# Gate products ahead of the query units in the NSA stage of a two-layer hybrid attention kernel

## The chip, the cores and the metric

The program runs on one core of one Trainium2 chip. The metric is the device time of one execution in microseconds (us), given as the median of several runs. The core's engines are TensorE (PE, matrix products; its weight loads are shown as PEld), VectorE (DVE), ScalarE (ACT), GpSimd (POOL) and SyncE (SP, which issues most of the loads). Each engine takes its own instructions strictly in order; semaphores between them are the only coupling.

## What is computed

Two decoder layers on a sequence of 512 tokens of width 1024, in float32. The part of a layer that the change touches:

```python
hn = rms_norm(x, norm_g[0])
(nsa_q, k_c, v_c, k_s, v_s, k_w, v_w, nsa_g, sb_q, sb_k, sb_v, merge_g) = split_columns(hn @ w_in)
kc = compress_blocks(k_c, ...); vc = compress_blocks(v_c, ...)      # gelu(flat @ w1) @ w2
y_nsa = nsa_attention(q_rope, q_plain, kc, vc, ks, vs, kw, vw, gates) @ w_nsa_o
y_sb  = stick_breaking_attention(sb_q, sb_k, sb_v) @ w_sb_o
gate  = jax.nn.sigmoid(merge_g)                                      # 2 * 1024 columns
mixed = (gate[..., :1024] * y_nsa + gate[..., 1024:] * y_sb) @ w_out
x = x + rms_norm(mixed, norm_g[1])
# then a feed-forward block: x = x + rms_norm(square(relu(h @ w_ff1)) @ w_ff2)
```

## The kernel before, in words

Activations lie transposed: 128 channels on the partitions, the 512 tokens along the row. Every float32 product is made of three float32r products: both operands are split into a high and a low part, and `three()` adds hi*hi, hi*lo and lo*hi in one PSUM bank. One output unit of 128 columns of `w_in` is therefore 8 input tiles x 3 = 24 matmuls of 128x512 (`product`, lines 479, 481, 483).

Each unit's weights are 512 KB. `Weight` (lines 145 to 170) loads them with SP into one of **two** raw buffers ("wr", line 149), ACT copies out the high part (L157), and the low part is made in one of two ways: POOL subtracts (L162), or, with `sub="dma"`, ACT writes the negative raw value into the low buffer as well (L159) and POOL issues an accumulating DMA of the same weights onto it (L160). High and low parts have four buffers each. A raw buffer is free again when its low part is made.

A layer runs in four stages. In the **NSA stage** PE works off an attention with small, dependent steps (scores L673/L674, transposes L720, values L735/L736), and a `Filler` puts independent matmuls between them: `fill.add` appends generators, `fill.run(n)` issues the next n filler steps, `fill.later(n, f)` calls f after n more steps, `fill.until(c)` issues steps until c holds. One step of a `product` is one matmul; one step of a compression unit (`ck.steps`, `cv.steps`, called C[0..3] and D[0..3] after `some(...)`, four steps each) is two matmuls of 64x256 (L378/L379). PE is scheduled by hand in exactly this order; the other engines' orders are made by a scheduler at build time.

The first scores wait for the keys K1, K2 (`keys`, L531 to L533) and the rotated queries xr (`queries`, then `stack`, L350/L351). The four score groups h = 0..3 come four heads at a time; two PSUM banks "s" hold them, so h = 2 needs the bank of h = 0 back, which DVE's masking step L679 frees. The filler before held, in this order (`ORD` number 2): C[0], query unit q2, C[1], q3, C[2], C[3], stick-breaking unit h0[0], D[0], D[1], h0[1], D[2], D[3], h0[2], the three units of h1, and the gate units of m = 0 and 1 (two each). 41 steps (`F0`) ran before the first scores. After C[3], `ck_done` sets off the chain of the compressed keys: transposes cmp_t (L389), DVE and ACT steps of a gelu (L392 to L400), the product cmp_o (L409).

The **stick-breaking stage** (L840 on) has the gate units m = 2..5 as filler. In the **merge stage** (L942 to L964) the remaining two pairs, m = 6 and 7, are issued at m = 1 (`GA`) and m = 4 (`GB`) as 48 filler steps each, between the units of the output projection. The feed-forward stage follows.

A gate product's result is multiplied by the norm factor on DVE (L642) into a tile "sig" that lives until the merge stage.

Of the kernel before, what the change touches and what calls it, by code (L numbers as in the profile page):

```python
# [25 lines left out]
P = 128  # L26
T = 512
D = 1024
# [21 lines left out]
def layer_kernel(ctx, tc, xT, pos, gvec, tri, consts, smalls, w_in, w1, w_o, w_out, ff1, ff2, out):  # L50
# [9 lines left out]
    BUFS = {"L": 20, "Q": 12, "P": 12, "pt": 4, "t": 4, "f": 4, "sig": 4, "act": 16, "st": 1, "R": 2}  # L60

    def big(tag, name, dt=F32):
        return sp.tile([P, T], dt, tag=tag, bufs=BUFS[tag], name=name)

# [406 lines left out]
    def layer(l, acts, R, heads):  # L471
# [165 lines left out]
        def gate_project(m):  # L637
            s2 = []

            def take(ps):  # L640
                s = big("L" if 2 <= m < 4 else "P" if 4 <= m < PLAN["GE"] else "sig", "sig")
                V.tensor_tensor(s, ps, R, ALU.mult)  # L642
                s2.append(s)
                sigs[m] = s2
# [154 lines left out]
        def some(gen, n=4):  # L799
# [12 lines left out]
        ORD = [  # L812
            [q2, C[0], q3, C[1], h0[0], C[2], C[3], h0[1], D[0], D[1], h0[2], D[2], D[3]],
            [q2, C[0], q3, C[1], C[2], h0[0], C[3], D[0], h0[1], D[1], D[2], h0[2], D[3]],
            [C[0], q2, C[1], q3, C[2], C[3], h0[0], D[0], D[1], h0[1], D[2], D[3], h0[2]],
            [q2, C[0], C[1], q3, C[2], C[3], h0[0], D[0], D[1], h0[1], D[2], D[3], h0[2]],
            [q2, C[0], h0[0], C[1], C[2], h0[1], C[3], D[0], q3, D[1], D[2], h0[2], D[3]],
            [h0[0], C[0], q2, C[1], C[2], h0[1], C[3], D[0], q3, D[1], D[2], h0[2], D[3]],
            [h0[0], C[0], q2, C[1], C[2], q3, C[3], D[0], h0[1], D[1], D[2], h0[2], D[3]],
        ][PLAN["ORD"]]  # L820
        fill.add(*ORD, *h1, *gate_project(0), *gate_project(1))
# [21 lines left out]
        fill.add(*(p for m in range(2, PLAN["GE"]) for p in gate_project(m)))  # L843
# [101 lines left out]
        for m in range(KT):  # L945
# [15 lines left out]
            for j in ((0, 1, 4, 5) if PLAN["GE"] == 4 else (0, 1, PLAN["GA"]) if PLAN["GE"] == 5 else (PLAN["GA"], PLAN["GB"])):  # L961
                if j == m:
                    fill.add(*gate_project(gates.pop(0)))
                    fill.run(48)  # L964
# [152 lines left out]
```

## Time and profile before

| | us |
|---|---|
| median of 3 runs | 1628.49 (1623.24 to 1630.78) |
| profiled execution, own time | 1626.38 |
| its span from first to last instruction | 1624.4 |
| PE busy | 1534.3 (94% of the span) |
| DVE busy | 870.5 (54%) |
| ACT busy | 747.9 (46%) |
| POOL busy | 768.2 (47%) |

The shares are averages over stages with different limits. PE's granted clock is 1.00 of full speed in most of the span and falls to half in a few short stretches. Times inside a stage are given from the span's start; layer 0's NSA stage begins at about 44 us, layer 1's at about 846 us, and the merge stages lie at about 350 to 405 us and 1150 to 1206 us.

### The profile page before, as it was taken

To read this page: it belongs to the slowest core of one execution; us is meant where nothing else is said; L and a number is where in the kernel's file an instruction comes from. 1 tells how busy PE (TensorE), PEld (TensorE's weight loads), DVE (VectorE), ACT (ScalarE), POOL (GpSimd) and SP (SyncE) were. 2 spreads that over 40 slices of the span, in tenths; PEclk is the share of its full clock that TensorE was granted. 3 is DMA by queue.
4 is the path that set the end of the run, shared out by engine and by line. 5 is a ranking of instruction groups with operands and counts; after the bars stand their busy time and mean duration, and the time that the engine had idled before them with its cause. 6 is when DMAs were issued, how large, how long until landed. Compare 5 with 4: busy or idle time off the path is not lost.

```text
span 1624.4 us, 20692 instructions
## 1 busy us (share of the span) xinstructions
PE 1534.3 (94%) x7810; PEld 1291.3 (79%) x7810; DVE 870.5 (54%) x1495; ACT 747.9 (46%) x1379; POOL 768.2 (47%) x527
## 2 busy tenths in 40 slices
PE   8788999999989999999887899999998999999996
PEld 5566778888988888888885777788878988888886
DVE  7877954354582332323799698534536823232245
ACT  6666755443352332324356677646343523232342
POOL 4762345446544444446546534354565344444452
PEclk9899999999999999999998999999999999999999
DMA  5464212224312322324234622122343133232321
GB/s 185 108 144 97 51 52 69 75 91 143 106 64 95 98 97 95 100 93 131 95 93 108 162 54 53 52 78 65 103 145 113 43 93 101 92 103 91 104 91 52
DMA packets 49331, 153.74 MB, mean 95 GB/s; under 512 B 5952, under 2 KB 12496, under 8 KB 49232
## 3 DMA queue, kind: packets, MB, share of 16 engines
q1 hardware_dynamic: 45888, 140.84, 27.2%
q0 software_dynamic: 3200, 11.55, 4.1%
q8 instruction: 61, 1.00, 0.3%
q14 instruction: 38, 0.31, 0.1%
q10 hardware_dynamic: 144, 0.03, 0.0%
HBM read 148.15 MB, written 4.26 MB: 94 GB/s over the span
## 4 chain that ended last, share of the span: by engine, by line
PE 77%; DVE 14%; ACT 3%; DMA 1%; issue 1%; POOL 0%; DVEq 0%; ACTq 0%; POOLq 0%
PE ff L186 12%; PE ff L185 12%; PE ff L187 12%; PE proj L483 5%; PE proj L479 5%; PE proj L481 5%; DVE P L690 2%; PE tail L187 2%; PE tail L186 2%; PE tail L185 2%; PE p_t L720 2%; DVE pn L291 2%; PE y L185 1%; PE y L187 1%; PE y L186 1%; PE head L185 1%
## 5 line engine op out<-in xcount | busy, mean ns | idle before, releaser
L162 POOL TENSOR_TENSOR w_lo<-w_raw,w_hi 128x1024 fp32r<-128x1024 f32 x204 | 496.7, 2435 | 503.2 <-ACT w_hi L157 483.5
L157 ACT ACTIVATE w_hi<-w_raw 128x1024 fp32r<-128x1024 f32 x226 | 239.1, 1059 | 530.0 <-PE ff L186 370.9
L483 PE MATMUL proj<-ah,w_lo 128*128 128x512 f32 x496 | 197.9, 399 | 1.7 <-POOL w_lo L162 1.7
L481 PE MATMUL proj<-al,w_hi 128*128 128x512 f32 x496 | 197.8, 399 | 0.0
L479 PE MATMUL proj<-ah,w_hi 128*128 128x512 f32 x496 | 196.8, 397 | 0.7 <-ACT w_hi L157 0.7
L185 PE MATMUL ff<-ah,w_hi 128*128 128x512 f32 x448 | 174.3, 389 | 0.0
L186 PE MATMUL ff<-al,w_hi 128*128 128x512 f32 x448 | 174.3, 389 | 0.0
L187 PE MATMUL ff<-ah,w_lo 128*128 128x512 f32 x448 | 174.3, 389 | 0.0
L186 PE MATMUL ff<-hl,w_hi 128*128 128x512 f32 x432 | 168.2, 389 | 0.8 <-DVE hl L181 0.8
L185 PE MATMUL ff<-hh,w_hi 128*128 128x512 f32 x432 | 168.1, 389 | 0.0
L187 PE MATMUL ff<-hh,w_lo 128*128 128x512 f32 x432 | 168.1, 389 | 0.0
L181 DVE TENSOR_TENSOR hl<-relu,hh 128x512 fp32r<-128x512 f32 x64 | 106.6, 1671 | 84.3 <-ACT hh L180 84.0
L483 PEld LDWEIGHTS proj<-ah,w_lo 128*128 128x128 f32 x496 | 94.1, 190 | 18.5 <-POOL w_lo L162 2.1
L479 PEld LDWEIGHTS proj<-ah,w_hi 128*128 128x128 f32 x496 | 94.0, 190 | 17.3 <-ACT w_hi L157 0.9
L481 PEld LDWEIGHTS proj<-al,w_hi 128*128 128x128 f32 x496 | 94.3, 190 | 16.7
L1012 DVE TENSOR_TENSOR ffa<-ff,ffa 128x512 f32<-128x512 f32 x38 | 26.3, 692 | 150.8 <-PE ff L187 150.8
L185 PEld LDWEIGHTS ff<-ah,w_hi 128*128 128x128 f32 x448 | 84.1, 188 | 17.5
L187 PEld LDWEIGHTS ff<-ah,w_lo 128*128 128x128 f32 x448 | 84.1, 188 | 17.5
L186 PEld LDWEIGHTS ff<-al,w_hi 128*128 128x128 f32 x448 | 84.1, 188 | 17.2
L186 PEld LDWEIGHTS ff<-hl,w_hi 128*128 128x128 f32 x432 | 81.1, 188 | 17.9 <-DVE hl L181 1.2
L185 PEld LDWEIGHTS ff<-hh,w_hi 128*128 128x128 f32 x432 | 81.1, 188 | 16.9
L187 PEld LDWEIGHTS ff<-hh,w_lo 128*128 128x128 f32 x432 | 81.1, 188 | 16.8
(311 smaller groups left out, 3431.1 us busy)
## 6 DMA issues: line engine op xcount, KB each, us to landing
w_raw<-in_ff_dram SPq DMA_DIRECT2D x128, 512.0 KB, 3.5
w_raw<-in_w_in_dram SPq DMA_DIRECT2D x69, 512.0 KB, 3.6
w_lo<-in_w_in_dram POOLq DMA_DIRECT2D x18, 512.0 KB, 7.5
w_raw<-in_w_dram SPq DMA_DIRECT2D x16, 512.0 KB, 3.5
w_raw<-in_w_o_dram SPq DMA_DIRECT2D x16, 512.0 KB, 3.5
w_raw<-in_w_out_dram SPq DMA_DIRECT2D x16, 512.0 KB, 3.5
x<-in_xT_dram SPq DMA_DIRECT2D x8, 256.0 KB, 6.5
w_lo<-in_w_dram POOLq DMA_DIRECT2D x4, 512.0 KB, 6.5
```

Source lines behind the costliest of these rows:

```text
L157: S.activation(h, raw, AF.Copy)
L162: (sub or G).tensor_tensor(l, raw, h.bitcast(F32), ALU.subtract)
L181: V.tensor_tensor(lo, src, hi.bitcast(F32), ALU.subtract)
L185: E.matmul(ps, w.hi(k), ah, start=first, stop=False)
L186: E.matmul(ps, w.hi(k), al, start=False, stop=False)
L187: return E.matmul(ps, w.lo(k), ah, start=False, stop=last)
L291: V.scalar_tensor_tensor(t, mixed[k][:, c], gcol(l, n, k), R[:, c], ALU.mult, ALU.mult)
L479: E.matmul(ps, w.hi(k), ah, start=(k == 0), stop=False)
L481: E.matmul(ps, w.hi(k), al, start=False, stop=False)
L483: E.matmul(ps, w.lo(k), ah, start=False, stop=(k == KT - 1))
L690: V.tensor_scalar(pr[h], pr[h], sm4[:, h:h + 1], None, ALU.mult)
L720: E.transpose(pt[:, P * h:P * h + P], pend[j][0][h][:, P * kt:P * kt + P], ident)
```

## The change

The order list is replaced by one fixed order, in which the first gate pair stands ahead of q2 and q3 in the NSA filler, and three gate pairs (m = 0, 1, 2) are in that stage instead of two. 76 filler steps instead of 41 run before the first scores; the items of query tiles 0, 1, 2 of the second head group get one step more each (`FN10` to `FN12`). The stick-breaking stage's filler has m = 3..6, and the merge stage issues one pair only, m = 7, at m = 1. Tiles "sig" get 6 buffers, and which pool a pair's tiles come from changes.

```diff
--- before.py
+++ after.py
@@ -15,9 +15,9 @@
 PSUM = bass.MemoryType.PSUM
 
 PLAN = {
-    "GE": 6, "GA": 1, "GB": 4,
-    "F0": 41, "F2": 5, "F3": 1, "F1": 7, "AH": 7, "BU": 2, "QD": 77, "FS0": 4, "FS1": 4, "FE": 5, "FN00": 5, "FN01": 3, "FN02": 4,
-    "FN03": 7, "FN10": 5, "FN11": 3, "FN12": 3, "FN13": 7, "FNC0": 1, "FNC1": 7, "CK0": 11, "CK1": 24, "CK2": 13,
+    "GE": 7, "GA": 1, "GB": 4,
+    "F0": 76, "F2": 5, "F3": 1, "F1": 7, "AH": 7, "BU": 2, "QD": 77, "FS0": 4, "FS1": 4, "FE": 5, "FN00": 5, "FN01": 3, "FN02": 4,
+    "FN03": 7, "FN10": 6, "FN11": 4, "FN12": 4, "FN13": 7, "FNC0": 1, "FNC1": 7, "CK0": 11, "CK1": 24, "CK2": 13,
     "CK3": 36, "CV0": 13, "CV1": 28, "SC3": 1, "SC2": 2, "R1": 3, "R2": 4, "CKV": 1, "CKM": 2, "CVM": 1, "ORD": 2, "HS": 6, "H0": 2, "HS2": 7, "FQ": 12,
     "CD": 0, "GT": 24,
 }
@@ -57,7 +57,7 @@
     dp = ctx.enter_context(tc.tile_pool(name="dp", bufs=1, space=bass.MemoryType.DRAM))
     xsave = dp.tile([P, KT, T], F32, name="xsave")
 
-    BUFS = {"L": 20, "Q": 12, "P": 12, "pt": 4, "t": 4, "f": 4, "sig": 4, "act": 16, "st": 1, "R": 2}
+    BUFS = {"L": 20, "Q": 12, "P": 12, "pt": 4, "t": 4, "f": 4, "sig": 6, "act": 16, "st": 1, "R": 2}
 
     def big(tag, name, dt=F32):
         return sp.tile([P, T], dt, tag=tag, bufs=BUFS[tag], name=name)
@@ -638,7 +638,7 @@
             s2 = []
 
             def take(ps):
-                s = big("L" if 2 <= m < 4 else "P" if 4 <= m < PLAN["GE"] else "sig", "sig")
+                s = big("L" if m in (3, 6) else "P" if m in (4, 5) else "sig", "sig")
                 V.tensor_tensor(s, ps, R, ALU.mult)
                 s2.append(s)
                 sigs[m] = s2
@@ -809,16 +809,8 @@
         values()
         q2, q3 = product(5, queries), product(6, last_query)
         C, D = [some(cks) for _ in range(4)], [some(cvs) for _ in range(4)]
-        ORD = [
-            [q2, C[0], q3, C[1], h0[0], C[2], C[3], h0[1], D[0], D[1], h0[2], D[2], D[3]],
-            [q2, C[0], q3, C[1], C[2], h0[0], C[3], D[0], h0[1], D[1], D[2], h0[2], D[3]],
-            [C[0], q2, C[1], q3, C[2], C[3], h0[0], D[0], D[1], h0[1], D[2], D[3], h0[2]],
-            [q2, C[0], C[1], q3, C[2], C[3], h0[0], D[0], D[1], h0[1], D[2], D[3], h0[2]],
-            [q2, C[0], h0[0], C[1], C[2], h0[1], C[3], D[0], q3, D[1], D[2], h0[2], D[3]],
-            [h0[0], C[0], q2, C[1], C[2], h0[1], C[3], D[0], q3, D[1], D[2], h0[2], D[3]],
-            [h0[0], C[0], q2, C[1], C[2], q3, C[3], D[0], h0[1], D[1], D[2], h0[2], D[3]],
-        ][PLAN["ORD"]]
-        fill.add(*ORD, *h1, *gate_project(0), *gate_project(1))
+        g0, g1, g2 = (gate_project(m) for m in range(3))
+        fill.add(g0[0], C[0], g0[1], C[1], q2, C[2], C[3], q3, D[0], D[1], h0[0], D[2], D[3], h0[1], g1[0], h0[2], g1[1], *g2, *h1)
         fill.later(PLAN["GT"], gate_rows)
         fill.run(PLAN["F0"])
         for h in range(4):
@@ -840,7 +832,7 @@
             nsa_values(it)
 
         fill.until(lambda: 0 in sb_in)
-        fill.add(*(p for m in range(2, PLAN["GE"]) for p in gate_project(m)))
+        fill.add(*(p for m in range(3, PLAN["GE"]) for p in gate_project(m)))
         blocks = [(h, kb) for h in range(4) for kb in (3, 2, 1, 0)]
         zs, sps, spt, accs, aps = {}, {}, {}, {}, {}
         loc = {0: (0, 0), 1: (1, 0), 3: (1, 384), 2: (2, 0)}
@@ -958,10 +950,9 @@
             mh, ml = big(tg, f"mh{m}", F32R), big(tg, f"ml{m}", F32R)
             split(mh, ml, sig[0])
             merged.append((mh, ml))
-            for j in ((0, 1, 4, 5) if PLAN["GE"] == 4 else (0, 1, PLAN["GA"]) if PLAN["GE"] == 5 else (PLAN["GA"], PLAN["GB"])):
-                if j == m:
-                    fill.add(*gate_project(gates.pop(0)))
-                    fill.run(48)
+            if m == PLAN["GA"]:
+                fill.add(*gate_project(gates.pop(0)))
+                fill.run(48)
         exp_table()
 
         mixed = [big("L", f"mix{m}") for m in range(KT)]
```

What it moves is seen on three places of two engines, all in layer 0; layer 1 has the same orders but for a few neighbours. Names: w_raw and w_hi are a unit's raw weights and high part, w_lo its low part; xr10, xr11 the rotated queries of the second pair of heads; V20, V21 the values; P_... the probabilities of one score group; cmp_hs the compressed keys' hidden layer.

ACT, from the keys to the values. Before, 615 is the high part of q3's weights and 683 that of C[2]'s; those of q2 and C[1] were made earlier:

```order
L533 ACTIVATE K2s_443<-K2s_443 64x512
L157 ACTIVATE w_hi_615<-w_raw_613 128x1024
L571 ACTIVATE qph_507<-q_493 128x512
L157 ACTIVATE w_hi_683<-w_raw_681 128x1024
L533 ACTIVATE K2w_444<-K2w_444 64x512
L350 ACTIVATE xr10_501<-qr_495 64x512
L350 ACTIVATE xr11_504<-qr_495 64x512
L543 ACTIVATE V20_445<-v_t_511 128x4x64
L543 ACTIVATE V21_446<-v_t_511 128x4x64
```

The same place in the change, where 618 and 619 are C[1]'s weights and 634 is the high part of q2's:

```order
L533 ACTIVATE K2s_443<-K2s_443 64x512
L157 ACTIVATE w_hi_618<-w_raw_616 128x1024
L159 ACTIVATE w_lo_619<-w_raw_616 128x1024
L571 ACTIVATE qph_507<-q_493 128x512
L533 ACTIVATE K2w_444<-K2w_444 64x512
L350 ACTIVATE xr10_501<-qr_495 64x512
L350 ACTIVATE xr11_504<-qr_495 64x512
L543 ACTIVATE V20_445<-v_t_511 128x4x64
L157 ACTIVATE w_hi_634<-w_raw_632 128x1024
L543 ACTIVATE V21_446<-v_t_511 128x4x64
```

C[1]'s low part, which goes by way of a POOL DMA, now starts behind the keys, and q2's weights behind xr10, xr11 and V20.

DVE, from the values to the first masking step L679, before:

```order
L544 TENSOR_TENSOR V21_446<-v_t_511,V21_446 128x4x64
L563 TENSOR_TENSOR q_579<-proj5_535,R0_104 128x512
L555 TENSOR_SCALAR gate_440<-gate_440 128x96
L342 STREAM_SHUFFLE rope_sh_582<-q_579 128x512
L556 RECIPROCAL gate_440<-gate_440 128x96
L344 TENSOR_TENSOR rope_sh_582<-rope_sh_582,sinT_331 128x512
L345 TENSOR_TENSOR qr_581<-qr_581,rope_sh_582 128x512
L679 ISA P_633,mx_628<-s_630,cst_68 128x512
```

and in the change:

```order
L642 TENSOR_TENSOR sig_552<-proj19_520,R0_104 128x512
L544 TENSOR_TENSOR V21_446<-v_t_511,V21_446 128x4x64
L555 TENSOR_SCALAR gate_440<-gate_440 128x96
L556 RECIPROCAL gate_440<-gate_440 128x96
L642 TENSOR_TENSOR sig_614<-proj20_582,R0_104 128x512
L679 ISA P_663,mx_658<-s_660,cst_68 128x512
```

The rotation of q2's queries (L342, L344, L345) has gone behind the first L679; two evacuations of gate products (L642) are in front of it.

ACT, a little later in the change, from q2's neighbours to the compressed keys' hidden layer (before, the weights of three units, C[3], h0[0] and D[0], stood between the values and cmp_hs, and two P_ and the rotated queries of q2):

```order
L157 ACTIVATE w_hi_690<-w_raw_688 128x1024
L157 ACTIVATE w_hi_710<-w_raw_708 128x1024
L157 ACTIVATE w_hi_727<-w_raw_725 128x1024
L157 ACTIVATE w_hi_821<-w_raw_819 128x1024
L681 ACTIVATE P_663,sm4_659<-P_663,mx_658 128x512
L159 ACTIVATE w_lo_822<-w_raw_819 128x1024
L571 ACTIVATE qph_684<-q_670 128x512
L157 ACTIVATE w_hi_842<-w_raw_840 128x1024
L681 ACTIVATE P_703,sm4_659<-P_703,mx_658 128x512
L382 ACTIVATE cmp_hs_722<-cmp_h_567 64x256
```

Weights of five units (C[2], C[3], q3, D[0], D[1]) now stand ahead of cmp_hs, which PE's transposes cmp_t wait for.

## Rows read from the trace of the kernel before

**Rows 1.** The page: busy us, share of the span, instructions of each engine.

```profile
PE 1534.3 (94%) x7810; PEld 1291.3 (79%) x7810; DVE 870.5 (54%) x1495; ACT 747.9 (46%) x1379; POOL 768.2 (47%) x527
```

**Rows 2.** PE timeline, layer 0: start us, us; in brackets idle before, releaser.

```profile
39.74 0.39 PE L479 MATMUL proj<-ah,w_hi 128*128 128x512 f32 x1
...
44.28 0.39 PE L483 MATMUL proj<-ah,w_lo 128*128 128x512 f32 x1
...
46.24 0.33 PE L378 MATMUL cmp_h<-w_hi,bhl 128*64 128x256 f32 x1 [1.13 <-ACT gts L519]
...
55.32 0.50 PE L479 MATMUL proj<-ah,w_hi 128*128 128x512 f32 x1 [0.65 <-ACT w_hi L157]
...
57.77 0.50 PE L483 MATMUL proj<-ah,w_lo 128*128 128x512 f32 x1 [1.71 <-POOL w_lo L162]
...
70.88 0.77 PE L673 MATMUL s<-K1s,xr 128*128 128x512 f32 x1 [7.14 <-ACT xr L350]
```

**Rows 3.** DVE timeline, layer 0.

```profile
63.52 0.42 DVE L544 TENSOR_TENSOR V<-v_t,V 128x256 fp32r<-128x256 f32 x1
...
70.05 0.68 DVE L679 CUSTOM_DVE_ANT_0 P<-s,cst 128x512 f32<-128x512 f32 x1
```

**Rows 4.** PE timeline, layer 1.

```profile
849.39 0.33 PE L378 MATMUL cmp_h<-w_hi,bhl 128*64 128x256 f32 x1 [2.33 <-DVE bhl L369]
...
860.91 0.50 PE L674 MATMUL s<-K2s,xr 128*128 128x512 f32 x1 [0.79 <-ACT K2s L533]
...
871.79 0.77 PE L673 MATMUL s<-K1s,xr 128*128 128x512 f32 x1 [6.73 <-DVE mx L679]
...
889.21 1.29 PE L720 MATMUL p_t<-cst,P 128*128 128x128 f32 x4 [2.26 <-DVE P L690]
...
898.29 0.79 PE L736 MATMUL o_nsa<-ptl,V 128*128 128x512 f32 x1 [3.58 <-DVE ptl L181]
```

**Rows 5.** Stretches: us, busy of PE, PEld, DVE, ACT, POOL, granted clock, DMA share, GB/s.

```profile
70.90:77.00 6.10, 6.10 (x23) 5.30 (x24) 5.96 (x10) 5.60 (x11) 4.08 (x3) 0.50 0.53 171
...
871.80:875.70 3.90, 3.90 (x15) 3.50 (x16) 3.70 (x6) 3.85 (x8) 2.18 (x1) 0.50 0.07 27
```

**Rows 6.** ACT timeline, layer 0.

```profile
54.21 1.06 ACT L157 ACTIVATE w_hi<-w_raw 128x1024 fp32r<-128x1024 f32 x1
...
61.31 0.39 ACT L543 ACTIVATE V<-v_t 128x256 fp32r<-128x256 f32 x1
```

**Rows 7.** POOL timeline, one row of each layer.

```profile
55.34 2.37 POOL L162 TENSOR_TENSOR w_lo<-w_raw,w_hi 128x1024 fp32r<-128x1024 f32 x1 [0.55 <-ACT w_hi L157]
...
854.37 1.28 POOL L343 TENSOR_TENSOR qr<-q,cosT 128x512 f32<-128x512 f32 x1 [2.77 <-DVE q L563]
```

**Rows 8.** Tile w_lo, POOL's DMAs issued in 40:50, then in 830:960.

```profile
DMA to landing us min/median/max: 7.5/7.5/7.5
...
DMA to landing us min/median/max: 5.4/7.2/8.9
```

**Rows 9.** The page's DMA issues: KB of each, median us to landing.

```profile
w_raw<-in_w_in_dram SPq DMA_DIRECT2D x69, 512.0 KB, 3.6
```

**Rows 10.** PE timeline, layer 0, around the compressed keys and values.

```profile
91.53 0.50 PE L736 MATMUL o_nsa<-ptl,V 128*128 128x512 f32 x1 [1.76 <-DVE ptl L181]
...
96.50 0.42 PE L409 MATMUL cmp_o<-cmp_ht,sml 128*64 128x32 f32 x4 [3.10 <-DVE ptl L181]
...
128.16 0.38 PE L415 MATMUL cmp_o<-sml,cmp_ht 128*32 128x64 f32 x4 [1.54 <-DVE cmp_ht L400]
...
130.38 0.49 PE L738 MATMUL o_nsa<-pth,vc 32*128 32x512 f32 x1 [1.84 <-DVE vc L418]
```

**Rows 11.** PE timeline, merge stage of layer 0, behind the second gate pair.

```profile
392.42 0.47 PE L185 MATMUL y<-onh,w_hi 128*128 128x512 f32 x1 [0.99 <-DVE sig L955]
```

**Rows 12.** DVE timeline, the same pair of operations in layers 0 and 1.

```profile
82.05 1.67 DVE L690 TENSOR_SCALAR P<-P,sm 128x512 f32<-128x512 f32 x2
...
881.76 7.79 DVE L690 TENSOR_SCALAR P<-P,sm 128x512 f32<-128x512 f32 x2
```

## The prediction

> **What bounds the kernel now.** The page's busy times come first [rows 1]: PE is busy 94% of the span, the next engine 54%. So the time is PE's work plus the gaps in it, and a change of order can only move gaps. The next view is PE's timeline in the NSA stage, read for the brackets, which name each gap and its releaser. In layer 0 the stage loses 1.13 us before the first compression unit, 0.65 and 1.71 us on q3's weights, and 7.14 us before the third score group [rows 2]; layer 1 loses 2.33, 0.79 and 6.73 us at the like places [rows 4]. The large one is the bank of the first group: it is free only when DVE has run L679, at 70.05 + 0.68 = 70.7 us, right where PE goes on at 70.88 [rows 2, 3]. In layer 0 the row names ACT's xr, which happened to end then; layer 1 names DVE's mx itself [rows 4]. DVE is late because q2's evacuation and rotation stand between the values (63.52) and L679 (70.05) [rows 3]. The view of stretches shows what such a gap costs afterwards: PE runs at half clock for 6.1 us behind it in layer 0 and for 3.9 us in layer 1 [rows 5], so half of that, 3.05 and 1.95 us, is lost on top.
>
> **The change, part by part.** *Steps moved.* From the first row to the last of 21 product matmuls PE takes (44.28 - 39.74) / 20 = 0.227 us each [rows 2]. One gate pair is 48 of them, 10.9 us. The merge stage loses one pair per layer, the NSA stage gains one, and the stick-breaking stage has eight products as before. PE's work is the same; what counts is how much of the 10.9 us falls into gaps that were there, and what gaps are new. 35 of the 48 steps go ahead of the first scores and 12 between later items.
>
> *Gaps that go.* The first gate product stands before C[0], so 24 x 0.227 = 5.4 us of work covers the 1.13 and 2.33 us. q2's rotation goes behind the first L679 on DVE; two evacuations of gate products take its place, and PE comes to the scores later, so the third group should find its bank free. Layer 0: 1.13 + 0.65 + 1.71 + 7.14 = 10.6 us, and 3.05 of half clock. Layer 1: 2.33 + 0.79 + 6.73 = 9.9 us, and 1.95.
>
> *New gap 1, C[1].* Its low part comes by a POOL DMA. Without its gap PE would have been at C[0] at 46.24 - 1.13 = 45.1 us; 48 gate steps, C[0] and the gate rows (some 1.7 us) bring it to C[1] at 57.7. On ACT C[1]'s high part stands where one was made at 54.21 [rows 6]; with that (1.06 us) and the copy of the low one (the same size of tile, so taken the same, overlapping a little) the DMA goes out at about 56.2. The one made nearest to it landed after 7.5 us [rows 8]: 63.7, a wait of 6.0 us. In layer 1 PE is there at 849.39 - 2.33 + 12.6 = 859.7; on POOL the DMA stands behind the rotation that ended at 855.6 [rows 7], and at layer 1's median of 7.2 us [rows 8] it lands at 862.8: 3.1 us. With landings from 5.4 to 8.9 us [rows 8] the bounds are 3.9 to 7.4 and 1.3 to 4.8. I take the middle values, each from its own layer.
>
> *New gap 2, half clock behind it.* The nearest rows are waits of 7.14 and 6.73 us, which cost 3.05 and 1.95 [rows 2, 4, 5]. For 6.0 us I take 2.0 and for 3.1 us 1.0; bounds 0 and 3.05.
>
> *New gap 3, the weights' ring and cmp_t.* Two raw buffers mean that a unit's load waits for the low part of the unit two before: 3.6 + 1.06 + 2.37 = 7.0 us for two units [rows 6, 7, 9]. q2's weights now stand behind the values on ACT: 61.31 + 0.39, then 1.06 and 2.37, so its low part is ready at 65.1. PE, through with C[1] at 64.5, hardly waits for it. C[2]'s low part follows at 68.7, C[3]'s at 72.1 and q3's at 75.7. D[1]'s raw load lands 3.6 later at 79.3, its high part is made by 80.4, and behind that stand one P_ and cmp_hs on ACT, about 1.2 us: PE's cmp_t gets its input at 81.6. PE ends its 76 steps at 65.1 + 20 x 0.227 = 69.6, with half clock 71.6; four score groups (8 matmuls) and 23 steps later, 7.0 us, it stands at cmp_t at 78.6. A wait of 3.0 us, taken for both layers since their queues stand alike; bounds 0 (PE is that much later anyway) and 5.
>
> *cmp_o.* It now stands ahead of the first transposes p_t. DVE has the same list to do before it (masks, two pairs of L690, the gelu). Before, PE lost 1.76 + 3.10 = 4.9 us around it in layer 0 [rows 10] and 2.26 + 3.58 = 5.8 in layer 1 [rows 4]. I take 4.9 for both: 0 and -0.9. It can be worse, which is the slow rival.
>
> *The compressed values.* Counted in filler steps behind the first scores their gelu comes at 128 + 13 - 41 = 100 before and 152 + 13 - 76 = 89 now: 11 steps, 2.5 us, earlier against gaps of 1.54 and 1.84 us [rows 10]. I take 2.5 off in layer 0 and nothing in layer 1, whose gaps there I leave as they are.
>
> *Costed at nothing.* Evacuations of the moved gate products: by the order DVE is through the values (63.52) and the gates some 3 us later and has nothing else to do until the scores; without that cover it is two evacuations, each of the size of L679 (0.68 us) [rows 3]. In the merge stage the pair at m = 4 goes with its 10.9 us. The gap of 0.99 us that followed it [rows 11] is a bank waiting for DVE's L955, and is as likely to stay as to go: 0 to -1 per layer. The weights there come one per unit before and after. The gates' two further buffers and the other pools change no wait that I find. The steps that are added between the later items of head group 1 lie where PE has hardly a gap; they cost their 12 x 0.227 us, which is in the sum already.
>
> **The sum.** Layer 0: -10.6 - 3.05 + 6.0 + 2.0 + 3.0 - 2.5 = -5.2. Layer 1: -9.9 - 1.95 + 3.1 + 1.0 + 3.0 - 0.9 = -5.6. Together -10.8 us. The profiled execution took 1626.38 us, so 1615.6; the median is 2.1 above that execution, which gives **1617.7 us**. By the bounds of gaps 1 and 3 this case reaches from 1610 to 1624. 0.5% of the median, about what a measurement can tell from no change, is 8.1 us: the border is at 1620.4.
>
> **A rule against it.** The pair of L690 took 1.67 us in layer 0 and 7.79 in layer 1 [rows 12], so something beside it can hold it up by 6.1 us. The Trainium skill, SBUF — State Buffer, section "SBUF: two separate sides", says that VectorE and GpSimd share a port pair by an exclusive lock: a GpSimd instruction that holds it blocks a two-port VectorE instruction to its end. The two rows agree with it as far as they go. By the bare rule each L690 that meets a weight split would wait up to that split's 2.37 us, and with all four pairs so held the sum would end at 1617.7 + 4 x 2 x 2.37 = 1636.7; I keep 1617.7, because the ring above gives POOL one split of 2.37 us in 3.5 us and so leaves gaps.
>
> **The rivals.**
> - *All the filler is cover* (0.20). C[1] lands as PE comes, and cmp_t and cmp_o find their inputs. Then both layers win the whole pair: 1626.4 - 2 x 10.9 + 2.1 = 1606.7. For it: the gaps that were there (10.6 + 3.05 us in layer 0) are larger than the pair. Against it: C[1]'s DMA can hardly start before 56 us [rows 6].
> - *One wait for another* (0.19). Landings at 8.9 us in layer 1 and likewise 1.4 us later in layer 0, half clock at 3.05 behind both, no gain at the compressed values and at cmp_o: +1.4 + 1.7 + 1.05 + 2.05 + 2.5 + 0.9 = 9.6 us of the 10.8 gone: 1627.3, no change. For it: each new gap stands where a chain of DMA, ACT and POOL has no slack.
> - *DVE is held up before cmp_o* (0.14). In the new order PE has nothing but cmp_o to go on with until DVE is through both pairs of L690 and the gelu. If all four pairs (two per layer) take 7.79 instead of 1.67 us, that is +24.5 us: 1642.2, slower. With three it is +7.6 against before, still within 0.5%; it decides from the fourth on. For it: POOL makes the weights of D[1] and h0[0] then. Against it: only one of the two rows of before shows it.
>
> **How the numbers follow.** The forecast has 0.47, about seven tenths of it (0.33) below 1620.4 and the rest (0.14) within 0.5%. With the rivals: faster 0.33 + 0.20 = 0.53, within 0.5% 0.14 + 0.19 = 0.33, slower 0.14. The range 1604 to 1634 leaves out the slow rival and the lower edge of the first one; the forecast's own range is 1610 to 1624.
>
> **What would show it.** Right: no gap before the third score group in either layer; a new one before C[1]'s first low matmul (L379), released by a DMA, of 4 to 7 us in layer 0 and about half in layer 1; one of some 3 us before cmp_t (L389), released by ACT; a merge stage shorter by 10.9 us with at most one gap of a microsecond. Wrong: a gap of 5 us or more before the third score group; no gap at C[1] (then the first rival); L690 pairs of 5 us and more with PE idle at cmp_o (then the slow one); or new gaps in the merge stage.

## The result, and the profile after

| | before | after |
|---|---|---|
| median us | 1628.01 (1623.24 to 1630.78, 4 runs) | 1609.39 (1607.93 to 1610.92, 4 runs) |
| profiled execution, own time / span | 1626.38 / 1624.4 | 1610.72 / 1608.8 |

The ratio is 0.9896, with a 95% interval of 0.9876 to 0.9916: 1.0% faster. Between the two profiled executions it is 15.7 us, and that difference is what the traces can explain. The stages, each from its first matmul to that of the next stage (values' transposes L540, first z of the stick-breaking stage, first product with w_out):

| us | before | after | difference |
|---|---|---|---|
| layer 0, NSA stage | 180.9 | 183.4 | +2.6 |
| layer 0, stick-breaking and merge | 172.6 | 166.4 | -6.2 |
| layer 1, NSA stage | 180.5 | 179.7 | -0.8 |
| layer 1, stick-breaking and merge | 175.5 | 164.5 | -11.0 |

With what stands ahead of the first stage and between the layers (+0.9 and -0.9) and -0.3 at the end, this is the difference of the spans. 10.9 us of gate products moved from the fourth row to the third and from the second to the first. So the NSA stage covered 10.9 - 2.6 = 8.3 us of them in layer 0 and all of them and 0.8 more in layer 1. The merge stage gave its 10.9 back in layer 1, but only 6.2 in layer 0. Layer 0 won 3.7 us, layer 1 11.8. A second execution of the same kernel ("After again" below) has 5.8 and 11.6, so a difference of 2 us in layer 0 lies within what one kernel does by itself.

The page after, against [rows 1]: PE's share of the span went from 94% to 95%. DVE was busy for 12 us less, POOL for 5 us less, and ACT as long as before.

```profile
PE 1528.3 (95%) x7810; PEld 1288.8 (80%) x7810; DVE 858.1 (53%) x1495; ACT 748.9 (47%) x1379; POOL 763.2 (47%) x527
```

The waits of PE after, whole span (engine, line, releaser: us in total, times, longest). C[1]'s low weights now head it, and all that waits at the scores' first line, L673, for DVE comes to 4.3 us:

```profile
PE cmp_h L379 <- DMA w_lo<-in_w_dram: 10.4, 3, 8.8
...
PE y L185 <- DVE sig L947: 6.3, 4, 2.4
...
PE s L673 <- DVE mx L679: 4.3, 6, 1.8
```

PE's timeline after, the gaps that the prediction speaks of, layer 0 first:

```profile
67.71 0.47 PE L379 MATMUL cmp_h<-w_lo,bhl 128*64 128x256 f32 x1 [8.83 <-DMA w_lo<-in_w_dram]
...
96.21 0.61 PE L409 MATMUL cmp_o<-cmp_ht,sml 128*64 128x32 f32 x4 [4.82 <-issue]
...
388.06 0.47 PE L185 MATMUL y<-onh,w_hi 128*128 128x512 f32 x1 [2.40 <-DVE sig L947]
...
858.01 0.50 PE L479 MATMUL proj<-ah,w_hi 128*128 128x512 f32 x1 [0.90 <-ACT w_hi L157]
860.45 0.80 PE L483 MATMUL proj<-ah,w_lo 128*128 128x512 f32 x1 [1.71 <-POOL w_lo L162]
875.24 0.34 PE L389 MATMUL cmp_t<-cst,cmp_hs 64*128 64x64 f32 x2 [0.65 <-ACT cmp_hs L382]
890.55 0.64 PE L409 MATMUL cmp_o<-cmp_ht,sml 128*64 128x32 f32 x4 [2.89 <-DVE cmp_ht L400]
```

The four gaps of [rows 2] and the three of [rows 4] up to the third score group are gone. In layer 0 there is one new gap, at C[1]; in layer 1 there is none at C[1], and a smaller one at q2's weights.

ACT's timeline after shows why the layers differ:

```profile
52.64 1.29 ACT L350 ACTIVATE xr<-qr 64x512 fp32r<-64x512 f32 x2 [6.42 <-DVE qr L345]
...
57.20 1.06 ACT L157 ACTIVATE w_hi<-w_raw 128x1024 fp32r<-128x1024 f32 x1
58.16 1.04 ACT L159 ACTIVATE w_lo<-w_raw 128x1024 fp32r<-128x1024 f32 x1
...
383.26 1.06 ACT L157 ACTIVATE w_hi<-w_raw 128x1024 fp32r<-128x1024 f32 x1 [4.84 <-DMA w_raw<-in_w_out_dram]
384.23 0.61 ACT L180 ACTIVATE mh<-sig 128x512 fp32r<-128x512 f32 x1
...
844.46 1.04 ACT L157 ACTIVATE w_hi<-w_raw 128x1024 fp32r<-128x1024 f32 x1
845.41 1.04 ACT L159 ACTIVATE w_lo<-w_raw 128x1024 fp32r<-128x1024 f32 x1
...
847.99 1.28 ACT L350 ACTIVATE xr<-qr 64x512 fp32r<-64x512 f32 x2 [0.93 <-DVE qr L345]
```

In layer 1 the two copies of C[1]'s weights stand ahead of the first xr (844.46, 847.99). In layer 0 they stand behind xr and the copies of the keys, and ACT had been idle for 6.42 us before that xr. What this does to C[1]'s DMA is read on POOL, whose timeline after is:

```profile
59.50 0.88 POOL L160 DMA_DIRECT2D w_lo<-in_w_dram  x1 [2.04 <-ACT w_lo L159]
...
81.50 2.69 POOL L162 TENSOR_TENSOR w_lo<-w_raw,w_hi 128x1024 fp32r<-128x1024 f32 x1
84.58 2.42 POOL L162 TENSOR_TENSOR w_lo<-w_raw,w_hi 128x1024 fp32r<-128x1024 f32 x1 [0.39 <-ACT w_hi L157]
...
384.40 2.37 POOL L162 TENSOR_TENSOR w_lo<-w_raw,w_hi 128x1024 fp32r<-128x1024 f32 x1 [2.96 <-ACT w_hi L157]
...
848.71 1.28 POOL L343 TENSOR_TENSOR qr<-q,cosT 128x512 f32<-128x512 f32 x1 [3.77 <-DVE q L563]
849.94 0.86 POOL L160 DMA_DIRECT2D w_lo<-in_w_dram  x1
```

C[1]'s DMA goes out at 59.50 in layer 0, 14.0 us behind the stage's start at 45.5, and at 849.94 in layer 1, 7.1 us behind its start at 842.9. In layer 0 it waited for ACT's copy; in layer 1 the copies were long there, and it went out right behind the rotation of q1 (L343). PE is at C[1] some 13 us behind either start.

DVE's timeline after carries the other two gaps:

```profile
46.11 3.88 DVE L344 TENSOR_TENSOR rope_sh<-rope_sh,sinT 128x512 f32<-128x512 f32 x1
...
53.30 1.40 DVE L351 TENSOR_TENSOR xr<-qr,xr 64x512 fp32r<-64x512 f32 x2 [0.70 <-ACT xr L350]
...
82.57 4.97 DVE L351 TENSOR_TENSOR xr<-qr,xr 64x512 fp32r<-64x512 f32 x2
...
94.87 1.24 DVE L400 TENSOR_TENSOR cmp_ht<-cmp_ht,cmp_u 128x64 f32<-128x64 f32 x1
...
384.87 2.45 DVE L181 TENSOR_TENSOR ml<-sig,mh 128x512 fp32r<-128x512 f32 x1 [2.88 <-ACT mh L180]
...
876.68 5.60 DVE L351 TENSOR_TENSOR xr<-qr,xr 64x512 fp32r<-64x512 f32 x2 [0.78 <-ACT xr L350]
```

The row before cmp_o says "issue", but L400, which makes its input, ends at 94.87 + 1.24 = 96.11 and PE goes on at 96.21: the wait is for DVE. DVE lost time there at the pair L351 of q2's queries, which took 4.97 and 5.60 us where q0's pair at 53.30 took 1.40. In the merge stage of layer 0 ACT's mh stands behind a copy that waits for a weight's DMA to land (383.26), DVE's L181 waits for mh, then takes 2.45 us, and L947 frees PE's bank only behind it.

### The profile page after: what moved, and what is told of

Same layout as the page of the kernel before. It is cut to its first block, busy times and chain, and to the rows that moved or that the text cites. A ratio compares the mean times of both kernels' runs of the same rounds, so it can differ in the third digit from the quotient of the medians.

```text
span 1608.8 us, 20693 instructions
## 1 busy us (share of the span) xinstructions
PE 1528.3 (95%) x7810; PEld 1288.8 (80%) x7810; DVE 858.1 (53%) x1495; ACT 748.9 (47%) x1379; POOL 763.2 (47%) x527
## 4 chain that ended last, share of the span: by engine, by line
PE 78%; DVE 12%; ACT 2%; issue 2%; DMA 1%; POOL 1%; DVEq 0%; ACTq 0%; POOLq 0%
PE ff L186 12%; PE ff L187 12%; PE ff L185 12%; PE proj L479 5%; PE proj L483 5%; PE proj L481 5%; PE tail L187 2%; PE tail L186 2%; PE tail L185 2%; PE y L185 2%; PE p_t L720 2%; DVE P L690 2%; PE y L186 2%; PE y L187 2%; DVE pn L291 2%
## 5 line engine op out<-in xcount | busy, mean ns | idle before, releaser
L162 POOL TENSOR_TENSOR w_lo<-w_raw,w_hi 128x1024 fp32r<-128x1024 f32 x204 | 494.6, 2425 | 506.1 <-ACT w_hi L157 493.6
L483 PE MATMUL proj<-ah,w_lo 128*128 128x512 f32 x496 | 198.7, 401 | 1.7 <-POOL w_lo L162 1.7
L479 PE MATMUL proj<-ah,w_hi 128*128 128x512 f32 x496 | 199.2, 402 | 0.9 <-ACT w_hi L157 0.9
L181 DVE TENSOR_TENSOR hl<-relu,hh 128x512 fp32r<-128x512 f32 x64 | 106.8, 1673 | 83.7 <-ACT hh L180 83.5
L483 PEld LDWEIGHTS proj<-ah,w_lo 128*128 128x128 f32 x496 | 94.8, 191 | 19.0 <-POOL w_lo L162 2.1
L479 PEld LDWEIGHTS proj<-ah,w_hi 128*128 128x128 f32 x496 | 95.0, 192 | 17.4 <-ACT w_hi L157 1.1
```

The costliest lines, as they stand in the source:

```text
L162: (sub or G).tensor_tensor(l, raw, h.bitcast(F32), ALU.subtract)
L181: V.tensor_tensor(lo, src, hi.bitcast(F32), ALU.subtract)
L479: E.matmul(ps, w.hi(k), ah, start=(k == 0), stop=False)
L483: E.matmul(ps, w.lo(k), ah, start=False, stop=(k == KT - 1))
```

## The experiments

All runs were compared with the kernel before on the same chip; ratios are to that. "After" is the changed kernel.

**The 35 steps taken back.**

```
-    "F0": 76,
+    "F0": 41,
```

> The changed kernel, but with 41 filler steps before the first scores instead of 76; the order of the filler and the three gate pairs stay. Theory A (the gain is PE's gap in front of the scores, filled by the 35 steps): PE comes to the scores some 8 us earlier than in the changed kernel, the keys and the rotated queries aren't there, and gaps of 4 to 8 us per layer come back in front of the score groups: 1617 to 1626 us. Theory B (the gain is the pair taken out of the merge stage, wherever its steps go): 1607 to 1612, as the changed kernel.

1615.03 us, 0.9931 (0.9910 to 0.9953): between the two ranges. So the 35 steps are worth about 5 us (this interval and after's just touch), and the rest of the gain doesn't need them. The gap of 7 us before the third group did not come back. In layer 1, where C[1] waits for nothing in this run either, that is the order's doing: L679 is through at 861.85, and the group waits 0.41 us. In layer 0 it isn't shown, because L679 ends at 66.43 and the wait at C[1] held PE until 67.03 anyway. What is new is a wait at the first o_nsa, the first product with the values, for DVE's ptl in both layers, and 1.22 and 1.53 us at the first scores of layer 1 (PE's timeline of this run):

```profile
67.03 0.47 PE L379 MATMUL cmp_h<-w_lo,bhl 128*64 128x256 f32 x1 [6.80 <-DMA w_lo<-in_w_dram]
...
88.48 0.79 PE L736 MATMUL o_nsa<-ptl,V 128*128 128x512 f32 x1 [3.26 <-DVE ptl L181]
...
862.01 0.47 PE L673 MATMUL s<-K1s,xr 128*128 128x512 f32 x1 [0.41 <-DVE mx L679]
```

**The order of before, with the 76 steps and the third pair.**

```
-        fill.add(g0[0], C[0], g0[1], C[1], q2, C[2], C[3], q3, ... g1[0], h0[2], g1[1], *g2, *h1)
+        fill.add(C[0], q2, C[1], q3, C[2], C[3], h0[0], D[0], D[1], h0[1], D[2], D[3], h0[2], *h1, *g0, *g1, *g2)
```

> The changed kernel with its 76 steps and three gate pairs in the NSA stage, but the filler in the order of before (C[0], q2, C[1], q3, C[2], C[3], h0..., all gate pairs last). Theory A1 (the order counts: q2's rotation has to go behind the first L679 on DVE): the third score group waits 5 us or more again in both layers, 1616 to 1624 us. Theory A2 (only the number of steps in front of the scores counts): that gap is under 2 us because PE comes 8 us later, and C[1]'s low part, whose DMA goes out at 44 us here, costs no gap: 1602 to 1610 us.

1627.62 us, 1.0002 (0.9992 to 1.0013): nothing is left of the gain, and the time lies above both ranges. The third group's gap did not come back, against theory A1: among PE's waits of this run there is none at L673. With 76 steps ahead of the scores DVE is through with q2's rotation before they come. The waits are now weights, late by way of DMA, POOL and ACT alike:

```profile
PE proj L483 <- DMA w_lo<-in_w_in_dram: 13.8, 4, 7.2
...
PE cmp_h L379 <- POOL w_lo L162: 5.7, 2, 3.1
...
PE proj L479 <- ACT w_hi L157: 4.0, 2, 3.4
```

A unit of compression uses up a weight in 4 steps, a product in 24. The first 76 steps of the old order take seven weights, those of the new one five: at 0.227 us a step one weight per 2.5 us and per 3.5 us. The ring of two raw buffers delivers one per 3.5 us by the prediction's working. So it is what stands between the compression units that lets the 76 steps be cover. That the ring's pace is the reason is worked out from these counts; no run with more raw buffers tested it.

**C[1]'s low part on POOL in place of the DMA.**

```
-    "CKM": 2,
+    "CKM": 0,
```

> The changed kernel with C[1]'s low part made by a subtraction on POOL instead of by a DMA. Theory: the 8.8 us gap before C[1]'s first low matmul in layer 0 is the DMA's landing; the subtraction takes 2.4 us from about 58.3, so the gap falls to 2 to 3 us, the half clock behind it goes, and 4 to 8 us are won in layer 0 and 0 to 1 in layer 1: 1602 to 1606 us. Rival (the ring of two raw buffers paces PE there): the wait comes back at q2's weights and at cmp_t, the time stays at 1608 to 1611.

1613.56 us, 0.9918 (0.9903 to 0.9933); no gain, and above both ranges. C[1]'s gap falls to 1.81 us, but PE waits at q2 and at cmp_t in its place (PE's timeline, layer 0):

```profile
65.54 0.77 PE L479 MATMUL proj<-ah,w_hi 128*128 128x512 f32 x1 [4.43 <-DVE sig L642]
...
83.58 0.33 PE L389 MATMUL cmp_t<-cst,cmp_hs 64*128 64x64 f32 x2 [2.92 <-ACT cmp_hs L382]
```

The first is new to the argument: q2's bank is one of the two that the gate products use, and DVE frees it when it gets to sig.

**The remaining pair of the merge stage at unit 4 in place of 1.**

```
-    "GE": 7, "GA": 1,
+    "GE": 7, "GA": 4,
```

> The changed kernel with the one gate pair of the merge stage at m = 4 instead of m = 1. The merge stage of layer 0 gave back 4.6 of 10.9 us (gaps of 1.0 and 2.6 us before y, and half clock behind). Theory: these gaps come from six units without a pair between them, in which DVE and ACT fall behind; with the pair at m = 4 the second gap goes and 1 to 4 us are won: 1605 to 1608 us. Rival: the gaps depend on the w_out and feed-forward weights that follow, and stay or move: 1608 to 1612.

1614.23 us, 0.9919 (0.9904 to 0.9934): no gain, and above both ranges. The gaps of layer 0's merge stage move to 354 us and shrink at its end, but don't go:

```profile
354.13 0.47 PE L185 MATMUL y<-onh,w_hi 128*128 128x512 f32 x1 [1.93 <-DVE sig L947]
...
389.80 0.47 PE L185 MATMUL y<-onh,w_hi 128*128 128x512 f32 x1 [1.12 <-DVE sig L947]
```

**After again, as the measure for the runs that follow.**

> The changed kernel as it is, a second time, as the measure for the two runs beside it. Both theories: 0.9896 of the kernel before, within 0.002 (1609 to 1612 us).

1609.47 us, 0.9904 (0.9886 to 0.9922). Its trace shows how far layer 0's gaps differ between two executions of one kernel (PE's timeline). C[1] waits 7.04 us in place of 8.83, because the DMA, out at 58.79, landed after 6.3 us and not after 8.2. Then cmp_t does wait, and the late gap of the merge stage is 2.76 us:

```profile
65.13 0.47 PE L379 MATMUL cmp_h<-w_lo,bhl 128*64 128x256 f32 x1 [7.04 <-DMA w_lo<-in_w_dram]
...
80.70 0.33 PE L389 MATMUL cmp_t<-cst,cmp_hs 64*128 64x64 f32 x2 [1.69 <-ACT cmp_hs L382]
...
386.80 0.47 PE L185 MATMUL y<-onh,w_hi 128*128 128x512 f32 x1 [2.76 <-DVE sig L947]
```

**Two pairs in the NSA stage, new order, 76 steps.**

```
-        g0, g1, g2 = (gate_project(m) for m in range(3))
+        g0, g1 = (gate_project(m) for m in range(2))
...
-            if m == PLAN["GA"]:
-                fill.add(*gate_project(gates.pop(0)))
-                fill.run(48)
+            for j in (PLAN["GA"], PLAN["GB"]):
+                if j == m:
+                    fill.add(*gate_project(gates.pop(0)))
+                    fill.run(48)
```

(with GE 6, FN10 to FN12 and the tiles of sig as before)

> The new order and the 76 steps with two gate pairs in the NSA stage instead of three (the third back in the merge stage at unit 4). Theory A, the third pair pays for the steps that were moved forward: 48 steps of filler are missing late in the NSA stage, so gaps come back there (NSA values and scores waiting for DVE and ACT) while the merge stage is 10.9 us longer per layer; 1620 to 1631 us, with the NSA stage shorter than after's by less than 5 us per layer. Theory B, the gain is the order's alone and the third pair only moves work: the NSA stage is shorter by the full 10.9 us per layer, no new gaps late in it, 1607 to 1613 us.

1611.74 us, 0.9918 (0.9899 to 0.9937), beside 0.9904 of after measured with it: the two intervals overlap, so the third pair is worth 2 us or nothing. The NSA stage is shorter than after's by 7.8 and 7.6 us, not by 10.9 and not by less than 5: 3 us of the pair are cover, and what is missing shows as small gaps, such as the wait before L673 at 181.38, 1.79 us against 0.7 in after. So the gain is mostly that of the order and the 35 steps. The order alone, with two pairs and 41 steps, was not run.

**C[1]'s copies ahead of xr on ACT.** Its weights go to tiles of P, which are free there, so ACT's order need not wait for a slot of the weights' rings.

```
+                    if sub == "dma":
+                        S.activation(self.l[j], raw[:, 512 * j:512 * j + 512], AF.Copy, scale=-1.0)
+                        nc.gpsimd.dma_start(self.l[j], src[:, 512 * j:512 * j + 512], accum_op=ALU.add)
+                        continue
...
-                w = Weight(w1[self.l, self.i, u], sub=...)
+                w = Weight(w1[self.l, self.i, u], "P" if (self.i, u) == (0, 1) else "w", sub=...)
```

> The second compression unit's weights of the keys are put into four tiles of P (its low part by two DMAs of 256 KB) instead of a slot of the rings wh and wl, so that ACT's order has their copies ahead of the first xr and not behind K2s. Theory A, the 8.8 us before C[1] in layer 0 come from where the copies stand on ACT: the DMAs go out some 10 us earlier, the gap and the half clock behind it (3.6 us) go, and 3 to 5 us of them come back at q2's weights or cmp_t: 1599 to 1606 us; layer 1, whose copies already stood ahead of xr, changes by under 3 us. Theory B, the wait only moves on to the next unit that has to come through the ring of raw buffers, as when POOL made that part: 1609 to 1614 us.

1606.28 us (1606.01 to 1607.43), 0.9885 (0.9863 to 0.9907); after, measured with it, 1609.47 (1607.83 to 1610.77). The spreads of times are 0.4 us apart but the ratios' intervals overlap, so a gain of 3 us is likely and not certain. The gap at C[1] is gone, although its two DMAs took longer to land than after's one, 9.5 us and more against 8.2: they went out at 46.3 and 46.8. This shows where the gap came from. A wait of 5.29 us takes its place at q2 (PE's timeline, layer 0; L483 and L413 of this kernel are L479 and L409 of after):

```profile
66.02 0.77 PE L483 MATMUL proj<-ah,w_hi 128*128 128x512 f32 x1 [5.29 <-DVE sig L646]
...
93.42 0.61 PE L413 MATMUL cmp_o<-cmp_ht,sml 128*64 128x32 f32 x4 [4.84 <-issue]
```

DVE's timeline of the same run has the evacuation that q2 waits for, ending at 65.88, and the pair of q2's queries, L355 here, at half the length that it has in after:

```profile
65.20 0.68 DVE L646 TENSOR_TENSOR sig<-proj,R 128x512 f32<-128x512 f32 x1
...
81.38 2.45 DVE L355 TENSOR_TENSOR xr<-qr,xr 64x512 fp32r<-64x512 f32 x2
```

**q2 in the other ring of banks, on top of it.**

```
-        q2, q3 = product(5, queries), product(6, last_query)
+        q2, q3 = product(5, queries, "o"), product(6, last_query)
```

> The run with C[1]'s copies ahead of xr, and besides q2's product in the ring of banks that q1 had (o), not in that of the gate products (d). Theory A, the wait that took the place of C[1]'s gap (5.45 us in layer 0, 1.93 us in layer 1, before q2's first matmul) is for the bank that DVE frees when it evacuates the first gate product, late in its list: both waits go with some 3 us of half clock, 1 to 4 us of it come back at cmp_t; 4 to 7 us under the run without this edit (1599 to 1602 us). Theory B, q2's weights or the scores' banks, which DVE frees too, are as late: within 2 us of it.

1607.25 us, 0.9889 (0.9868 to 0.9911): within 1 us of the run before it. The wait for sig goes, and the first scores come at 64.7 us in place of 73.4. Yet cmp_o starts at the same time as without the edit (PE's timeline, layer 0):

```profile
80.74 0.34 PE L393 MATMUL cmp_t<-cst,cmp_hs 64*128 64x64 f32 x2 [1.67 <-ACT cmp_hs L386]
...
93.46 0.39 PE L413 MATMUL cmp_o<-cmp_ht,sml 128*64 128x32 f32 x4 [3.23 <-issue]
```

93.42 and 93.46: what PE gains ahead of cmp_o is waited away by cmp_o. The same holds for cmp_t (80.69 and 80.74). So these times are not set by PE but by what releases it: ACT's list of weights with cmp_hs behind it, then DVE's list.

**cmp_o 21 steps later.**

```
-    "CK1": 24,
+    "CK1": 45,
```

> The changed kernel with cmp_o 21 filler steps later (CK1 45 for 24; compressed scores and softmax of group 0 move with it). Theory A, the 4.8 us (layer 0) and 2.9 us (layer 1) before cmp_o are only because it stands ahead of work that PE could do while DVE, held up at xr (4.97 and 5.60 us), gets to the gelu: both gaps go with the half clock behind them (3.4 us each) and nothing is late for the later step; 1600 to 1605 us. Theory B, PE is short of ready work there: p_t waits for DVE's L690 in its place, or the softmax of group 0 is late; 1607 to 1612 us.

1624.46 us, 0.9996 (0.9983 to 1.0009): nearly the whole gain is lost, more than theory B allowed. The wait stands at the first o_nsa (PE's timeline, layer 0), and the compressed scores behind cmp_o are late too; the NSA stages are 5.9 and 7.6 us longer than after's (189.3 us in layer 0).

```profile
101.30 0.79 PE L736 MATMUL o_nsa<-ptl,V 128*128 128x512 f32 x1 [5.64 <-DVE ptl L181]
```

**Both.** The edits of the last two, with C[1]'s copies ahead.

> Both edits together, with C[1]'s copies ahead. If the waits are independent the two gains add: 1609.5 - 3 - (4 to 7) - (5 to 9) = 1590 to 1597 us. If cmp_o's wait only grows or shrinks with what PE gained before it, the second edit gives what the first took: 1598 to 1604 us.

1619.26 us, 0.9965 (0.9948 to 0.9982): above both ranges. They don't add; o_nsa waits 5.54 us for ptl here as well.

**Eight more steps ahead of cmp_o, cmp_o itself unmoved**, on the run with C[1]'s copies ahead.

```
-    "F2": 5, "CK1": 24,
+    "F2": 7, "CK1": 32,
```

> The run with C[1]'s copies ahead of xr (1606.3 us), with 8 more filler steps between the scores of the second group (F2 7 for 5), and CK1 32 for 24 so that cmp_o stays where it was against the scores. Theory A, cmp_o's time is set by DVE's list and the last waits there (5.0 and 3.4 us) are free room for filler that has slack later (the 48 steps of the third pair were worth only 2 us): 8 steps of 0.227 us, 1.8 us per layer, are won: 1602 to 1604 us. Theory B, the steps pull weights forward that are not there yet, or are missing later: 1606 to 1610 us.

1604.35 us (1602.97 to 1605.88), 0.9868 (0.9846 to 0.9891), the fastest of all: below every time of the run without the 8 steps. But that run was on another chip, and the ratios' intervals overlap, so 2 us are not certain. Between the two traces the NSA stages are 0.9 and 1.1 us shorter, of the 1.8 expected. In layer 0 cmp_o's wait falls from 4.84 to 1.23 us (PE's timeline), and waits of up to 2.51 us at o_nsa take some of that back:

```profile
92.75 0.39 PE L413 MATMUL cmp_o<-cmp_ht,sml 128*64 128x32 f32 x4 [1.23 <-issue]
```

**Sixteen more.** F2 9, CK1 40.

> The same with 16 steps (F2 9, CK1 40). Theory A: 3.6 us per layer, as long as cmp_o's wait is longer than that: 1598 to 1602 us. Theory B: no better than with 8 steps, 1605 us or more.

1612.15 us, 0.9918 (0.9898 to 0.9938): the steps that go forward now reach a product whose weights are not there (PE's timeline, layer 1). As far as these two runs show, the first 8 steps were paid for by slack and the next 8 were not.

```profile
900.16 0.50 PE L487 MATMUL proj<-ah,w_lo 128*128 128x512 f32 x1 [3.86 <-DMA w_lo<-in_w_in_dram]
```

## Why the prediction was right, and where it was not

It said faster, with 1617.7 us as the likeliest and 1604 to 1634 as the range. 1609.4 lies in the range, 0.6 below the end of the forecast's own 1610 to 1624. Layer 0 went as the forecast had it, 3.7 us against 5.2. Layer 1 went as the rival had it in which all the filler is cover: 11.8 us against that rival's 10.9 and the forecast's 5.6. So the time is right partly because errors cancel: the gap at C[1] was longer than forecast in layer 0 and none in layer 1, and the one at cmp_t nearly didn't come.

- *Gaps that go*: right in both layers, 10.6 and 9.9 us and the half clock behind them. Two runs refine the reason. The third group's gap goes by the order alone (the run with 41 steps, layer 1) and also by the 76 steps alone (the run with the old order). The 35 steps are cover for waits that otherwise stand at o_nsa.
- *New gap 1, C[1]*: right in place and releaser in layer 0, too small in size: 8.83 us against 6.0 and its bounds of 3.9 to 7.4. The DMA went out at 59.50, not 56.2, and landed after 8.2 us, not 7.5: 4.0 us later than forecast, while PE came 1.2 later. Of the 3.3 us of the start, 1.0 is the stage's own (45.46 against 44.51). The rest is DVE's: L344 took 3.88 us at 46.11, so qr, xr and ACT's copies behind them slipped. The landing differs between executions: with 6.3 us in the second one the gap was 7.04 us and inside the bounds. That ACT's order is the cause is shown by the run that put layer 0's copies ahead: no gap.
- *The same step in layer 1* failed: 3.1 us were forecast, and C[1] waits for nothing. The DMA does stand right behind the rotation on POOL, as the text has it. But the text took the rotation's time from before, 855.6, which is 9.2 us behind the stage's start; after, it ended 7.1 us behind it (849.99 against 842.89). The q that it waits for (DVE's L563) came 2.2 us sooner counted so: before, an L344 ahead of it took 2.88 us at 849.26 beside a split on POOL; after, 0.68. And the DMA landed after 5.3 us, not 7.2: at 855.2, 0.9 us ahead of PE. Either alone would have left about 1 us of the wait.
- *New gap 2, half clock*: 3.6 us at half in layer 0, the first row below, so 1.8 lost; 2.0 was forecast. In layer 1 it is not at C[1] but at q2's weights, with 6.2 us at half (the third row), 3.1 lost against 1.0. The columns are those of [rows 5].

```profile
67.70:71.30 3.60, 3.59 (x12) 3.20 (x13) 0.00 (x0) 1.06 (x1) 1.37 (x2) 0.50 0.59 216
96.20:102.10 5.90, 5.89 (x21) 4.87 (x22) 4.76 (x5) 1.64 (x4) 5.90 (x4) 0.50 0.31 94
860.40:866.60 6.20, 6.15 (x15) 4.82 (x16) 5.03 (x7) 2.91 (x7) 4.21 (x2) 0.50 0.51 165
```

- *New gap 3, cmp_t*: no gap in layer 0 and 0.65 us in layer 1, for 3.0 each. The chain of weights was right: cmp_hs ended at 81.53 in layer 0, for 81.6. What failed is PE's time. The lower bound held, for the reason given with it: PE was later, by C[1]'s wait in layer 0 and by the waits and half clock at q2's weights in layer 1. Where these are shorter the gap appears: 1.69 us in layer 0 of the second execution, 1.67 there in the run with q2's bank, and 3.04 in layer 1 of the run with C[1]'s copies ahead, in which PE ran at full clock from the stage's start up to there.
- *cmp_o*: 4.82 us in layer 0 for 4.9, and 2.89 in layer 1 for 4.9; layer 1 has 1.77 us more before a score that waits for the same hold-up on DVE (883.07). Behind the first PE ran 5.9 us at half clock (the second row above; 3.4 us in before), which the step left out.
- *What holds DVE up ahead of cmp_o* is not what the text named. Only one of the two pairs of L690 stands ahead of cmp_o, and it took 2.02 us in either layer; q2's L351 took 4.97 and 5.60. The pair of layer 0 ended at 87.54, 0.5 us behind the second of two splits on POOL, the subtractions L162 (84.58 + 2.42 = 87.00). In the run with C[1]'s copies ahead the second split begins only at 83.68, as the pair ends, and the pair took 2.45. There cmp_o came 2.5 us earlier (93.42 - 45.14 against 96.21 - 45.46) counted from the stage's start, though not by the pair alone: the pair began 0.9 us earlier, and a small DVE operation behind it took 1.3 us longer. So L351 ends with the splits that run beside it; no run took the splits alone away. The Trainium skill, SBUF — State Buffer, section "Who interferes with whom", has a sentence that the prediction should have gone by: a VectorE instruction with two inputs in SBUF contends with a GpSimd instruction that reads SBUF. L351 has two such inputs (qr and xr), and these rows agree with it. The hold-up was priced on L690 instead, which reads one tile and a column. L690 can be held up as well, as the 7.79 us of [rows 12] show, beside POOL's work without a break from 881.74 to 888.86; here its pair ahead of cmp_o met less of it.
- *Costed at nothing, gate evacuations*: right only because C[1]'s gap covers them. With that gap gone q2 waits 5.29 us for sig, which is at the end of a list of rotation, keys and values on DVE. The text had DVE with "nothing else to do" there.
- *The compressed values*: right. Of layer 0's gaps of 1.54 and 1.84 us one of 0.97 is left, so 2.4 us are gone for 2.5; layer 1 has 0.97 for 0.90.
- *Costed at nothing, merge stage*: layer 1's sum is right, but not for the reason given. Both layers have a new gap of 0.85 us early in the stage and one of over 2 us late in it. In layer 0 the late one is 2.40 us in place of the 0.99 of [rows 11], with 3.4 us at half clock behind it: about 4 us came back. In layer 1 it is 2.16 us and was 2.24. There the clock made up for the 0.85: the kernel before ran 3.4 us at half clock behind this gap (first row below), after at full clock (second row). In its second execution after has full clock behind layer 0's gap too (third row), although that gap is longer. So the half clock here is luck of the execution. Layer 0's late gap grew because PE came to it 5.8 us earlier (385.66 against 391.43) and the chain that it waits for, from the weight that ACT copies, only 4.3 (383.26 against 387.58).

```profile
1196.60:1200.00 3.40, 3.40 (x10) 2.65 (x9) 1.91 (x3) 1.58 (x2) 1.17 (x2) 0.50 0.61 197
...
1181.50:1187.00 5.50, 5.47 (x24) 4.58 (x25) 3.47 (x4) 1.98 (x3) 3.26 (x3) 1.00 0.51 182
...
386.80:392.30 5.50, 5.50 (x24) 4.58 (x25) 3.44 (x4) 1.75 (x3) 3.25 (x3) 1.00 0.52 180
```

- *Rivals*: one wait for another holds in part of layer 0. In the run with the old order it is the outcome, though with waits for weights in general. The slow one did not come: DVE was held up ahead of cmp_o, but at L351 and by some 4 us per layer. Its price had an error besides: the pair of layer 1 already took 7.79 us before, so by its own figures three pairs were left to add, 18.4 us, and these would have ended within 0.5%.
- *The signs*: of those for right, the third score group's holds in both layers, and C[1]'s in layer 0 in place and releaser, but not in size. Two of those for wrong came: no gap at C[1] in layer 1, and new gaps in the merge stage.

## What to carry to other kernels

Filler that is put ahead of a stage is cover only as fast as its weights come: count weights per step in the first stretch, against what the ring of raw buffers delivers. Here the same 76 steps were worth some 17 us more (0.9896 against 1.0002) with products between the small units than with the units close together. Where an engine runs its list in order, read where the copies of the next weight stand in that list in each layer by itself; the scheduler may order two layers differently. And before taking a gap away, look which chain sets the next meeting point: here two runs had cmp_o at the same time, although PE was earlier in one of them.

## What the runs showed of the hardware

Three kinds of DVE operation with both inputs in SBUF took about three and a half to six times as long beside POOL's: L351 as a pair 1.40 us with POOL idle, 4.97 and 5.60 beside two splits; L344 3.88 us at 46.11, while POOL worked on until 49.4, where one at 58.82 took 0.69; L181 2.45 us beside the split at 384.40, where one at 390.93 took 0.69. Each ended 0.5 to 0.6 us behind the POOL operation that ran beside it. None of them waits for that operation's result, so the opening's remark that semaphores are the only coupling of the engines does not hold for DVE and POOL. A weight's low part by POOL's DMA landed 8.2 us after its issue at 59.50, 6.3 us after it at the same place of the second execution, and 5.3 us after the issue at 849.94, while SP's plain loads of the same 512 KB have a median of 3.6 us [rows 9]. Gaps of 2.2 to 2.8 us before PE's y were followed by half clock in some executions (0.50 for 3.4 us behind 2.40 us at 388.06) and not in others (1.00 behind 2.76 us at 386.80).
